# Both attentions of a hybrid transformer block: transposes of the inverted sums placed behind the products with the values

## The chip, the cores and the metric

The kernel runs on one core of a Trainium2 chip. The metric is the device time of one execution in microseconds (us); the time before is the median of three runs. A profile of one execution comes with it. Its engines are TensorE (PE for matmuls, PEld for the loading of their weights), VectorE (DVE), ScalarE (ACT), GpSimd (POOL) and SyncE (SP, which here only issues DMAs). Every engine works through its own queue in the order of the program and waits at an instruction until what it needs is there.

## What is computed

A transformer block on 1024 tokens of width 1024, with 256 context tokens, all in float32. After a norm and one wide projection there are two attentions with 8 heads of width 64 each, whose results are gated, projected and added to the input; a mixture of 16 experts follows.

```python
def _attend(q, k, v, scale):                       # latent attention, all 1280 keys
    s = jnp.einsum('bqhd,bkhd->bhqk', q, k).astype(jnp.float32) * scale
    p = jax.nn.softmax(s, axis=-1).astype(v.dtype)
    return jnp.einsum('bhqk,bkhd->bqhd', p, v)
...
# local attention: a window of 8 x 16 tokens on a 16 x 64 grid, and the context
p = jax.nn.softmax(jnp.concatenate([s_loc, s_ctx], axis=-1), axis=-1).astype(v.dtype)
return (jnp.einsum('bhqk,bqkhd->bqhd', p[..., :nk], v_win)
        + jnp.einsum('bhqk,bkhd->bqhd', p[..., nk:], v_ctx))
```

Both softmaxes are left undivided in the kernel: the products with the values run on the bare exponentials, and their result is multiplied by the inverse of the sums.

## The kernel before

The program is written out by hand in the order in which each engine shall take it. Its stages are: norm and input projections (to about 480 us), the local attention (`na_attention`, to about 662 us), the latent attention (`ml_attention`, to about 940 us), output projection with gates, norm and router, and the experts (from about 1180 us).

Both attentions go over 64 units; a unit is one head and 128 queries. Unit n's scores stand in a score tile (`pS`, two of them). `soft` takes their maximum on VectorE (L767 to L773 in the local attention, L887 to L889 in the latent one) and the exponential on ScalarE (L775; L891 and L892), which also gives the row sum. `transp` brings the exponentials (queries by keys) into keys by queries: 128x128 transposes on TensorE into tiles `pT` and `pY`, from which ScalarE (L788, L800, L802; L912) and, for the last two key blocks of the latent attention, VectorE (L914) evacuate them. `pv` multiplies with the values: the output has the head's 64 columns as partitions and the queries as columns, so two heads stand one above the other in one tile (64-column weights; L815 local, L927 latent).

The scale of a query is then needed as a row, the same on 64 partitions. For that `inverses` takes the reciprocal of the sums and spreads each over 64 columns on VectorE (L716, L718); `rows_of` transposes this on TensorE (L724) into spare columns of the products' own tile, and ScalarE copies the result back to the buffer `inv` (L725), by which VectorE multiplies the products (L819 local, L934 latent).

One step n of either loop issues: the inverses (every fourth step), the scores of unit n + 2, the transposes of unit n, every fourth step `pv` for the four units before, the rest of the evacuations, `soft` of unit n + 2, and the scaling. In the local attention a fourth step has two `pv` of a pair of units each, the first into the tile `pM`, the second into `pY`; in the latent attention it has one `pv` for two heads and 256 queries, into `pY`, of which there is one buffer and which the last transposes of the other three units use too. `pv` puts the transposes of the inverses first, then the products; the copy stands behind the products in the program of the local attention and ahead of them in the latent one.

The last step of the latent attention (n = 64) has no unit of its own. What follows on ScalarE is the first split of the projection (`split`, L86, with its remainder on VectorE, L87): weights and attention results are each parted into a rounded value and a remainder. The gated products of the projection are taken on VectorE (L1157); the loads of gates (L1086, L1087) and of the next weights (L1014) stand behind one another in SP's queue.

Of the kernel before, what the change touches and what calls it, by code (L numbers as in the profile page):

```python
# [9 lines left out]
F32 = mybir.dt.float32  # L10
# [17 lines left out]
def block_kernel(ctx, tc, a, out, dbg=None):  # L28
# [6 lines left out]
    def pool(st, name, side=None, **kw):  # L35
        return st.enter_context(tc.tile_pool(name=name, bufs=kw.pop("bufs", 1), side=side, reuse_waits="tile", **kw))
# [37 lines left out]
    def ps_S():  # L74
        return psum[0].tile([128, psum[4]], F32, name="pS", bufs=psum[1])

    def ps_T():
        return psum[0].tile([128, 512], F32, name="pT", bufs=psum[2])

    def ps_Y():  # L80
        return psum[0].tile([128, 512], F32, name="pY", bufs=psum[3])
# [7 lines left out]
    def mm3(ps, ahi, alo, bhi, blo, first, last):  # L89
        nc.tensor.matmul(ps, ahi, bhi, start=first, stop=False)  # L90
        nc.tensor.matmul(ps, ahi, blo, start=False, stop=False)  # L91
        nc.tensor.matmul(ps, alo, bhi, start=False, stop=last)  # L92
# [564 lines left out]
    for it, (kind, c) in enumerate(order):  # L657
# [4 lines left out]
        n = T if kind in "qg" else N  # L662
# [43 lines left out]
    yp = pool(yst, "y", side="right")  # L706
# [7 lines left out]
    def inverses(r, n):  # L714

        nc.vector.reciprocal(r, r)  # L716
        w = p.tile([128, n, 64], F32, name=f"inv{n}", bufs=2)
        nc.vector.tensor_copy(w, r[:, :, None].to_broadcast([128, n, 64]))  # L718
        return w.rearrange("p n c -> p (n c)")

    def rows_of(w, ps, dst=None):

        for i in range(0, w.shape[1], 128):
            nc.tensor.transpose(ps[:, i:i + 128], w[:, i:i + 128], ident)  # L724
        return lambda: nc.scalar.activation(w if dst is None else dst, ps, AF.Copy)  # L725
# [4 lines left out]
    def ps_M():  # L730
        return psum[0].tile([128, 512], F32, name="pM")

    def na_attention(then):

        units = [(2 * c + h, j) for c in range(4) for j in range(8) for h in range(2)]
        S, Pm, PT, RS, PT2 = {}, {}, {}, {}, {}

        def geo(j):
            R0 = min(max(2 * j - 4, 0), 8)
            rows = 9 if 2 <= j <= 5 else 8  # L740
            return R0, rows
# [62 lines left out]
        def pv(n0, inv):  # L804

            c, j = units[n0][0] // 2, units[n0][1]
            R0, rows = geo(j)
            py = ps_Y() if n0 % 4 else ps_M()
            copy = rows_of(inv, py[:, 128:256])
            kts = [8, 9] + [R0 // 2 + i for i in range(4)] + ([R0 // 2 + 4] if rows == 9 else [])  # L810
            for i, kt in enumerate(kts):
                kk = 64 if i == 6 else 128
                for h in range(2):
                    col = (2 * c + h) * 64
                    nc.tensor.matmul(py[h * 64:(h + 1) * 64, 0:128], vna[0:kk, kt, col:col + 64],  # L815
                                     PT[n0 + h][0:kk, i], start=(i == 0), stop=(i == len(kts) - 1))
            PT.pop(n0), PT.pop(n0 + 1)
            copy()
            return lambda: nc.vector.tensor_tensor(yT[:, 4 + c, j * 128:(j + 1) * 128], py[:, 0:128], inv, op=OP.mult)  # L819

        nu = len(units)
# [43 lines left out]
    def ml_attention():  # L865
        units = [(2 * c + h, 2 * g + i) for c in range(4) for g in range(4) for h in range(2) for i in range(2)]
        S, Pm, PT, RS = {}, {}, {}, {}

        def score(n):
            h, j = units[n]  # L870
            o = heads[8 + h]
            ps = ps_S()
            smid[0] = smid[0] or ps_M()
            mid = smid[0][:, (n % 2) * 256:(n % 2 + 1) * 256]
            q = slice(j * 128, (j + 1) * 128)
            for c0, c1 in ((0, 512), (512, 1024), (1024, N)):
                mm3(ps[:, c0:c1] if c0 < 1024 else mid, o["qh"][:, q], o["ql"][:, q], o["kh"][:, c0:c1], o["kl"][:, c0:c1], True, True)
            S[n] = ps, mid

        def soft(n):  # L880
            ps, mid = S.pop(n)
            sm = p.tile([128, 3], F32, name="sn", bufs=6)
            g, h, i = n // 4, n // 2 % 2, n % 2
            if n % 4 == 0:
                RS[g] = p.tile([128, 2, 4], F32, name="st", bufs=3)
            total = RS[g][:, :, 2 * i + h:2 * i + h + 1]
            nc.vector.tensor_reduce(sm[:, 0:1], ps, axis=AX.X, op=OP.max)  # L887
            nc.vector.tensor_reduce(sm[:, 1:2], mid, axis=AX.X, op=OP.max)
            nc.vector.tensor_scalar(sm[:, 2:3], sm[:, 0:1], sm[:, 1:2], -MLA_SCALE, op0=OP.max, op1=OP.mult)  # L889
            pm = p.tile([128, N], F32, name="pm", bufs=3)  # L890
            nc.scalar.activation(pm[:, T:], mid, AF.Exp, bias=sm[:, 2:3], scale=MLA_SCALE, accum_out=total[:, 0])  # L891
            nc.scalar.activation(pm[:, :T], ps, AF.Exp, bias=sm[:, 2:3], scale=MLA_SCALE, accum_out=total[:, 1])  # L892
            Pm[n] = pm

        tb = {}

        def transp(n, b):
            tb[b] = ps_Y() if b == 2 and (n % 4 or n == 0) else ps_T()
            k0, k1 = ((0, 4), (4, 8), (8, 10))[b]
            for k in range(k0, k1):  # L900
                nc.tensor.transpose(tb[b][:, (k - k0) * 128:(k - k0 + 1) * 128], Pm[n][:, k * 128:(k + 1) * 128], ident)  # L901

        def evac(n, b):
            g, i = divmod(n, 4)
            h = i // 2
            if b == 0 and i % 2 == 0:
                PT[g, h] = p.tile([128, 2560], F32, name="pt", bufs=4).rearrange("p (k q) -> p k q", q=256)
            k0, k1 = ((0, 4), (4, 8), (8, 10))[b]
            dst = PT[g, h][:, k0:k1, (i % 2) * 128:(i % 2 + 1) * 128]
            src = tb.pop(b)[:, :(k1 - k0) * 128].rearrange("p (k q) -> p k q", q=128)  # L910
            if b < 2:
                nc.scalar.activation(dst, src, AF.Copy)  # L912
            else:
                nc.vector.tensor_copy(dst, src)  # L914

        py = [None]

        def pv(g):
            c = g // 4
            py[0] = ps_Y()  # L920
            dst = RS[g] if g < 15 else yp.tile([128, 256], F32, name="inv")
            rows_of(RS[g], py[0][:, 256:512], dst)()
            RS[g] = dst
            for k in range(10):
                for h in range(2):
                    col = (2 * c + h) * 64
                    nc.tensor.matmul(py[0][h * 64:(h + 1) * 64, 0:256], vm[:, k, col:col + 64], PT[g, h][:, k],  # L927
                                     start=(k == 0), stop=(k == 9))

        def scaled(g):  # L930

            r, y, c = RS.pop(g), py[0], g // 4
            PT.pop((g, 0)), PT.pop((g, 1))
            return lambda: nc.vector.tensor_tensor(yT[:, c, (g % 4) * 256:(g % 4 + 1) * 256], y[:, 0:256], r, op=OP.mult)  # L934

        def start(n):
            score(n)
            soft(n)

        na_attention(start)  # L940
        if "yna" in dbg:
            nc.sync.dma_start(dbg["yna"], yT[:, 4:8])
        nu = len(units)
        for n in range(nu + 1):
            on = 0 <= n < nu
            if on:
                c, i = divmod(n, 16)
                if i in (0, 7) and c < 3:
                    todo.extend(ml_prep(2 * c + 2 + (i == 7)))
                if n + 2 < nu and units[n + 2][0] // 2 != units[n][0] // 2:  # L950
                    while todo:
                        todo.pop(0)()
            if n >= 4 and n % 4 == 0:
                r = RS[n // 4 - 1]
                nc.vector.tensor_tensor(r[:, 0], r[:, 0], r[:, 1], op=OP.add)
                RS[n // 4 - 1] = inverses(r[:, 0], 4)
            if n + 2 < nu:
                score(n + 2)
            if on:
                for b in range(2):  # L960
                    transp(n, b)
                    evac(n, b)
            out = None
            if n >= 4 and n % 4 == 0:
                pv(n // 4 - 1)
                out = scaled(n // 4 - 1)
            if on:
                transp(n, 2)
            if n + 2 < nu:
                soft(n + 2)  # L970
            if on:
                evac(n, 2)
                Pm.pop(n)
            if out:
                last.append(out)
                if n // 4 - 1 < 15:
                    last.pop()()
            if todo:
                todo.pop(0)()
# [977 lines left out]
```

## Time and profile before

| | us |
|---|---|
| median of three runs | 1809.28 (1805.93, 1809.28, 1815.73) |
| the profiled execution | 1804.39 |
| its span, first to last instruction | 1802.6 |
| TensorE busy in the span | 1682.8 (93%) |
| VectorE busy | 1176.6 (65%) |
| ScalarE busy | 927.9 (51%) |
| GpSimd busy | 596.4 (33%) |
| local attention | about 484 to 662 |
| latent attention | about 664 to 940 |

Matmuls are pipelined and their ends are modelled, so a busy TensorE is not TensorE at its peak. The share of busy time is an average over stages with different limits; what a change in one stage is worth is read in that stage. In the rows below, a bracket at the end of a row of the timeline gives the time for which the engine sat idle before it, and what ended that; rows of several like instructions are merged and carry their count.

### The profile page before, as it was taken

How to read it: one execution, taken by the hardware profiler on the slowest of the kernel's cores; microseconds unless marked ns; L12 is line 12 of the kernel's file. 1: busy time of each engine (PE TensorE's matmuls, PEld its weight loads, DVE VectorE, ACT ScalarE, POOL GpSimd, SP SyncE). 2: the span in 40 equal slices, each digit the busy share in tenths (PEclk: the TensorE clock that was granted, in tenths of full speed). 3: DMA queues.
4: the chain of work that ended last, by engine and by line, in shares of the span. 5: the costliest groups of instructions: out<-in, count | busy, mean ns of one | idle time of the engine just before them, and what ended most of it. 6: DMA issues, size and time to landing. Idle time of an engine off the chain costs nothing. (4 is left out here: it accounts for less than half of the span.)

```text
span 1802.6 us, 25426 instructions
## 1 busy us (share of the span) xinstructions
PE 1682.8 (93%) x9607; PEld 1340.9 (74%) x9609; DVE 1176.6 (65%) x1860; ACT 927.9 (51%) x1477; POOL 596.4 (33%) x488
## 2 busy tenths in 40 slices
PE   5999999999899999999989999788999999999996
PEld 3778778897777777777767776546887887888872
DVE  5612143203477766656555587887999999999986
ACT  3422222112366666667670032245777777777774
POOL 0334555543244422112000101256333433443135
PEclk9999999999999999999999999889999999999998
DMA  8334545255334311000025643877999999999944
GB/s 327 108 115 142 214 164 204 85 133 145 102 80 87 72 36 40 21 21 21 1 82 159 211 164 152 319 286 272 367 380 370 392 388 379 374 387 394 369 163 187
DMA packets 96891, 356.63 MB, mean 198 GB/s; under 512 B 28368, under 2 KB 36944, under 8 KB 70912
## 3 DMA queue, kind: packets, MB, share of 16 engines
q1 hardware_dynamic: 78032, 285.78, 43.9%
q0 software_dynamic: 11376, 41.42, 7.7%
q10 hardware_dynamic: 7360, 27.81, 3.9%
q8 instruction: 75, 1.23, 0.3%
q14 instruction: 48, 0.39, 0.1%
HBM read 312.85 MB, written 42.12 MB: 197 GB/s over the span
## 5 line engine op out<-in xcount | busy, mean ns | idle before, releaser
L1711 DVE TENSOR_TENSOR hl<-raw,hl 128x1024 fp32r<-128x1024 f32 x177 | 214.8, 1241 | 21.8 <-ACT hl L1710 19.9
L1710 ACT ACTIVATE hl<-raw 128x1024 fp32r<-128x1024 f32 x182 | 187.9, 1057 | 39.8 <-PE pgate L92 19.2
L405 PE MATMUL pS<-uhi,whi 128*128 128x512 f32 (+1 forms) x440 | 131.0, 386 | 2.9 <-DVE stg L492 2.2
L1607 POOL TENSOR_SCALAR oh<-iot,slot 128x128 bf16<-128x128 f32 x112 | 133.3, 1206 | 0.5
L87 DVE TENSOR_TENSOR wlo<-raw,whi 128x1024 fp32r<-128x1024 f32 x25 | 35.8, 1434 | 145.5 <-ACT whi L86 145.5
L405 PE MATMUL pS<-uhi,wlo 128*128 128x512 f32 (+1 forms) x440 | 129.3, 383 | 0.0
L405 PE MATMUL pS<-ulo,whi 128*128 128x512 f32 (+1 forms) x440 | 129.1, 382 | 0.0
L310 POOL TENSOR_TENSOR sb<-qs,sa 128x512 fp32r<-128x512 f32 x28 | 35.9, 1283 | 265.3 <-DVE sa L309 132.9
L1710 ACT ACTIVATE whl<-raw 128x1024 fp32r<-128x1024 f32 x91 | 96.5, 1060 | 39.3 <-PE pgate L92 19.0
L1864 POOL DMA_INDIRECT acc_d<-ye,idx x15 | 35.1, 2341 | 243.1 <-DVE ye L1858 243.1
L1711 DVE TENSOR_TENSOR whl<-raw,whl 128x1024 fp32r<-128x1024 f32 x88 | 108.5, 1233 | 9.1 <-ACT whl L1710 7.8
L1711 DVE TENSOR_TENSOR raw<-raw 128x1024 fp32r<-128x1024 f32 x89 | 108.8, 1223 | 6.1 <-ACT raw L1710 6.0
L912 ACT ACTIVATE pt<-pT 128x512 f32<-128x512 f32 x128 | 69.5, 595 | 81.6 <-PE pT L901 78.4
L380 POOL TENSOR_TENSOR rawm<-rawm,scol 128x1024 f32<-128x1024 f32 x32 | 65.5, 2048 | 132.1 <-DMA rawm<-in_w_mod_dram 132.1
L1710 ACT ACTIVATE raw<-raw 128x1024 fp32r<-128x1024 f32 x91 | 96.3, 1058 | 19.8 <-PE pup L92 7.3
L1237 PE MATMUL pS<-raw,hl 128*128 128x512 f32 x384 | 96.0, 399 | 1.6 <-DVE t L1157 1.1
L887 DVE TENSOR_REDUCE sn<-pS 128x1 f32<-128x1024 f32 x64 | 78.3, 1223 | 27.7 <-PE pS L92 27.1
L405 PEld LDWEIGHTS pS<-uhi,whi 128*128 128x128 f32 x440 | 79.1, 189 | 22.8 <-issue 3.9
L405 PEld LDWEIGHTS pS<-uhi,wlo 128*128 128x128 f32 x440 | 80.4, 189 | 16.3
L405 PEld LDWEIGHTS pS<-ulo,whi 128*128 128x128 f32 x440 | 80.2, 188 | 16.5
L927 PE MATMUL pY<-pt,v 128*64 128x256 f32 x640 | 72.6, 382 | 10.5 <-ACT inv L725 10.5
L1237 PEld LDWEIGHTS pS<-raw,hl 128*128 128x128 f32 x384 | 69.7, 188 | 16.9 <-ACT cb L1329 1.5
(493 smaller groups left out, 4688.6 us busy)
## 6 DMA issues: line engine op xcount, KB each, us to landing
raw<-in_w_exp_gate_dram SPq DMA_DIRECT2D x64, 1024.0 KB
raw<-in_w_exp_up_dram SPq DMA_DIRECT2D x64, 1024.0 KB
raw<-in_w_exp_down_dram SPq DMA_DIRECT2D x64, 1024.0 KB
rawm<-in_w_mod_dram POOLq DMA_DIRECT2D x32, 512.0 KB, 3.9
raw<-in_w_in_dram SPq DMA_DIRECT2D x25, 512.0 KB
wm<-in_w_mod_dram SPq DMA_DIRECT2D x8, 1024.0 KB
sig_d<-stg ACTq DMA_DIRECT2D x16, 512.0 KB
sg<-sig_d SPq DMA_DIRECT2D x32, 256.0 KB
```

Source lines behind the costliest of these rows:

```text
L87: eng.tensor_tensor(lo, src, hi.bitcast(F32), op=OP.subtract)
L310: lo_engine[0].tensor_tensor(lo[:, cs], src[p0:p1, cs], hi[p0:p1, cs].bitcast(F32), op=OP.subtract)
L380: nc.gpsimd.tensor_tensor(raw, raw, scol[:, :, 0:1].to_broadcast([128, KT, 128]), op=OP.mult)
L405: nc.tensor.matmul(pt[:, c0:c1], ww[:, kt], uu[:, kt, c0:c1], start=(kt == 0 and k == 0), stop=(kt == KT - 1 and k == 2))
L887: nc.vector.tensor_reduce(sm[:, 0:1], ps, axis=AX.X, op=OP.max)
L912: nc.scalar.activation(dst, src, AF.Copy)
L927: nc.tensor.matmul(py[0][h * 64:(h + 1) * 64, 0:256], vm[:, k, col:col + 64], PT[g, h][:, k], start=(k == 0), stop=(k == 9))
L1237: nc.tensor.matmul(ps[b], x[:, kt], w[:, kt % 4], start=(kt == 0 and k == 0), stop=(kt == 7 and k == 2))
L1607: nc.gpsimd.tensor_scalar(ohb[:, t], iot, slot[:, t, e:e + 1], None, op0=OP.is_equal)
L1710: nc.scalar.activation(w[:, 0], src, AF.Copy)
L1711: lo_on(e, i).tensor_tensor(w[:, 1], src, w[:, 0].bitcast(F32), op=OP.subtract)
L1864: nc.gpsimd.indirect_dma_start(out=acc_d[:, :], out_offset=bass.IndirectOffsetOnAxis(ap=idx[:, :1], axis=0), in_=ye, in_offset=None, compu ...
```

## The change

In the local attention the transposes of the inverses move from ahead of a pair's products to behind them; the copy stays behind both. In the latent attention the transposes move behind the products too, and the copy, which stood between transposes and products, moves to the end of the step: behind `soft` of unit n + 2 and the evacuation L914, just ahead of the scaling. No instruction is added or removed.

```diff
@@ na_attention, pv
             py = ps_Y() if n0 % 4 else ps_M()
-            copy = rows_of(inv, py[:, 128:256])
...
             PT.pop(n0), PT.pop(n0 + 1)
-            copy()
+            rows_of(inv, py[:, 128:256])()
@@ ml_attention, pv
             py[0] = ps_Y()
-            dst = RS[g] if g < 15 else yp.tile([128, 256], F32, name="inv")
-            rows_of(RS[g], py[0][:, 256:512], dst)()
-            RS[g] = dst
             for k in range(10):
...
+            dst = RS[g] if g < 15 else yp.tile([128, 256], F32, name="inv")
+            copy = rows_of(RS[g], py[0][:, 256:512], dst)
+            RS[g] = dst
+            return copy
@@ ml_attention, step n
-                pv(n // 4 - 1)
+                copy = pv(n // 4 - 1)
                 out = scaled(n // 4 - 1)
...
             if out:
+                copy()
                 last.append(out)
```

## Rows read from the trace of the kernel before

**Rows 1.** Both attentions: stretch, its length, busy time (count) per engine, clock, DMA.

```profile
484.00:662.00 178.00, 162.43 (x1619) 136.53 (x1618) 133.43 (x364) 120.28 (x309) 71.03 (x49) 1.00 0.32 69
664.00:934.00 270.00, 255.44 (x1837) 204.83 (x1835) 164.67 (x339) 179.23 (x399) 44.37 (x34) 1.00 0.10 28
```

**Rows 2.** Waits, latent attention: engine, tile, line, releaser; us in all, times, longest.

```profile
PEld pY L927 <- ACT inv L725: 13.6, 15, 1.0
...
PE pY L927 <- ACT inv L725: 10.0, 15, 0.8
...
PEld pY L724 <- PE pT L901: 3.3, 6, 0.6
```

**Rows 3.** Timeline, one group: start, us, engine, line, operation, idle before and its releaser.

```profile
800.38 1.22 DVE L887 TENSOR_REDUCE sn<-pS 128x1 f32<-128x1024 f32 x1
...
801.18 1.08 ACT L912 ACTIVATE pt<-pT 128x512 f32<-128x512 f32 x2
801.30 0.25 PEld L724 LDWEIGHTS pY<-ident,inv 128*128 128x128 f32 x2
...
802.15 0.39 ACT L725 ACTIVATE inv<-pY 128x256 f32<-128x256 f32 x1
...
802.59 4.08 PEld L927 LDWEIGHTS pY<-pt,v 128*64 128x64 f32 x40 [1.03 <-ACT inv L725]
...
802.86 1.14 ACT L892 ACTIVATE pm<-pS,sn 128x1024 f32<-128x1024 f32 x1
...
807.06 0.20 PEld L901 LDWEIGHTS pT<-ident,pm 128*128 128x128 f32 x2 [0.39 <-issue]
...
807.53 0.43 DVE L914 COPY pt<-pT 128x256 f32<-128x256 f32 x1 [5.34 <-PE pT L901]
...
807.87 0.41 DVE L934 TENSOR_TENSOR yT<-pY,inv 128x256 f32<-128x256 f32 x1
...
809.85 0.25 PEld L901 LDWEIGHTS pY<-ident,pm 128*128 128x128 f32 x2
```

**Rows 4.** Waits of TensorE in the local attention.

```profile
PE pM L724 <- DVE inv L718: 5.8, 5, 1.3
PE pS L754 <- ACT pm L775: 5.8, 22, 0.4
...
PE pY L724 <- DVE inv L718: 1.1, 3, 0.4
```

**Rows 5.** Timeline of one step with products in the local attention.

```profile
581.60 0.33 PE L724 MATMUL pM<-ident,inv 128*128 128x128 f32 x1 [1.21 <-DVE inv L718]
...
585.09 0.15 DVE L773 TENSOR_SCALAR sm<-sm 128x1 f32<-128x1 f32 x1
...
585.47 0.19 PEld L754 LDWEIGHTS pS<-sc,sa 128*128 128x128 f32 x1 [0.17 <-issue]
...
585.59 0.28 ACT L725 ACTIVATE inv<-pY 128x128 f32<-128x128 f32 x1 [1.88 <-PE pY L815]
...
586.18 0.94 ACT L775 ACTIVATE pm<-pS,sm 128x832 f32<-128x832 f32 x1
...
587.27 0.19 PEld L754 LDWEIGHTS pS<-sc,sa 128*128 128x128 f32 x1 [0.27 <-ACT pm L775]
```

**Rows 6.** Timeline, last group of the latent attention and start of the projection.

```profile
934.17 0.42 DVE L914 COPY pt<-pY 128x256 f32<-128x256 f32 x1 [2.24 <-PE pY L901]
...
936.07 0.62 ACT L86 ACTIVATE hl<-raw 128x512 fp32r<-128x512 f32 x1
...
936.23 4.08 PEld L927 LDWEIGHTS pY<-pt,v 128*64 128x64 f32 x40 [0.71 <-ACT inv L725]
...
936.73 0.69 DVE L87 TENSOR_TENSOR hl<-raw,hl 128x512 fp32r<-128x512 f32 x1 [1.52 <-ACT hl L86]
```

**Rows 7.** The chain that ended last, at the projection's start: start, us, what.

```profile
950.25 1.15 DVE t L1157
...
954.63 6.81 DMA raw<-in_w_proj_dram
```


## The prediction

> **What bounds the kernel now.** I read the stretches first: what each engine does in the local attention (the loop over `na_attention`, about 484 to 662 us) and in the latent attention (`ml_attention`, 664 to 934 us). In both TensorE is the busiest engine by far, 162.4 of 178 us and 255.4 of 270 us, always at the full granted clock [rows 1]. So a gain must come out of TensorE's 14.6 us of idle time in the second stretch and 15.6 us in the first; nothing in the change takes work from it. Then the list of waits tells what TensorE idles for, and the timeline of one group shows the order of the steps.
>
> In the latent attention nearly all of it stands at one place. Fifteen times the weight loads of the values' product (L927) wait for ScalarE's copy of the inverted sums (L725), 13.6 us in all (the matmuls' own idle time is put at 10.0, but their ends are modelled, and weight loads show when the queue went on, so I count those); six times the transposes of the sums (L724) also come late, 3.3 us of weight-load gap, because VectorE has not yet spread the inverses [rows 2]. One group shows it: the two transposes of the sums are issued at 801.30, right behind the unit's own; ScalarE is busy with the two evacuations L912 until 802.26 and takes the copy at 802.15, and only at 802.59 do the products start, after 1.03 us without a weight load [rows 3].
>
> In the local attention TensorE idles for two things: for VectorE's spread inverses (5.8 us in five places, 1.1 us in three), and 5.8 us in 22 places because the next scores (L754) need a score tile that ScalarE's exponential (L775) has not yet released [rows 4]. Its units run almost as fast as ScalarE allows.
>
> **The change, latent attention.** Nothing is removed: 16 groups keep their two transposes, one copy and 40 product passes. The products now stand first. What they read, the probabilities of the four units before, was evacuated in the step before, so they can start when the unit's own transposes have been issued. The gap of 13.6 + 3.3 = 16.9 us [rows 2] goes, except for what TensorE takes to change from a whole 128-column array to 64-column halves. That change is not visible ahead of the product today, since it lies inside the wait. Its nearest rows are the other way round: 0.17 us after 128-column products [rows 5] and 0.39 us after 256-column ones [rows 3]. The transposes before the product have 128 columns, so I take 0.17: 15 x 0.17 = 2.6, and 16.9 - 2.6 = **14 us** for the fifteen groups inside the loop. Bounds: 16.9 with no drain, 16.9 - 15 x 0.39 = 11 with the long one. The switch behind the product is paid once now (to the transposes of the unit) and once after (to the transposes of the sums).
>
> *A rule weighed here.* The products write other columns of the tile than the copy reads, and still they begin 0.05 us after its end (802.54 to 802.59) [rows 3]. The Trainium skill, "PSUM — Partial Sum Buffer", section "PSUM bank collisions raise a hardware error", says that two engines must be kept apart by bank and not by address; the trace agrees, and by that rule the new order has no such wait left, as ScalarE reads the bank after TensorE's last write. Against the change speaks "TensorEngine Tiling (Array Packing)", section "Key Properties" of the Trainium skill: changing the tiling mode drains TensorE. By it every switch costs a drain of what is in flight, which is the first rival below.
>
> What the copy's new place costs: ScalarE takes it behind the exponentials of the unit after next. Those run until about 804.0, and the product's end is near 806.7 today [rows 3], some 0.9 us earlier afterwards, so ScalarE is idle when the transposes of the sums come, and the copy follows them by about 0.4 us. On VectorE, L914 comes first and takes 0.43 us after the unit's last transposes, as now; the scaling L934 then finds the copy done (transposes, then 0.39 us of copy, against transposes, L914's wait and its 0.43). L934 frees the tile pY, the only buffer of its kind, for the next unit's last transposes, and ends at 808.28, 1.57 us before they start [rows 3]. Queued behind L934 on VectorE are the next unit's maxima, which wait for scores anyway. Cost: none, hidden by that 1.57 us. SP's and POOL's queues are not passed: no DMA belongs to the moved step.
>
> **The change, local attention.** The wait for the inverses, 5.8 + 1.1 = 6.9 us [rows 4], moves behind a product of some 2 us, where the inverses are ready. But what is late next? In three of the five places the two waits stand together, as 1.21 us at 581.60 and some 0.37 us more at the second transpose (a third of the 1.1 [rows 4]). There VectorE is late itself: its last step for the next exponential, L773, ends at 585.24, and the exponential starts at 586.18 [rows 5]. It can move up by 0.94 us, not by 1.58. So three places give 3 x 0.94 = 2.8, the others the rest, 6.9 - 3 x 1.58 = 2.2: 5.0 us. Against it: the second copy now waits for a transpose that stands behind the second product. Today the copy starts 0.12 us after the scores that follow (585.59 against 585.47). Afterwards the transpose ends 0.33 us after its start, of which its weight load (half of the 0.25 us for two [rows 3]) lies ahead of the scores, and the copy follows: about 0.24 us. These 0.12 us go into the chain copy, evacuations, exponential, release of the score tile, on which TensorE waits for 0.27 us already [rows 5]: 16 x 0.12 = 1.9 us. Net **3 us** gained; bounds -1.9 and +6.9.
>
> **The change, last group.** Its copy stands at the end of ScalarE's work for the attention, ahead of the splits for the projection (L86). Today the copy is taken before the product, and L86 starts at 936.07 while TensorE multiplies. Afterwards the product starts when L914 has ended (934.59), takes 4.08 us of weight loads and the 0.39 us of switching, to 939.1; transposes and copy take about 0.7 us more, and L86 starts near 939.8: 3.7 us later [rows 6]. VectorE follows ScalarE's first split without a gap until the first gated product L1157 at 950.25, and that stands on the chain that ended last: from it SP's queue goes on to the load of the next projection weights at 954.63 [rows 7]. So the last group **loses 3.8 us** on the path, with nothing to hide it (0 if the projection had slack, which the chain denies).
>
> **Sum.** -14 - 3 + 3.8 = -13.4 us (rounded from 3.1). The profiled execution has 1804.4 us (span 1802.6), so 1791.0. The median of the three runs is 1809.3, 4.9 us above the profiled one: on that scale 1796. Behind the projection everything waits for what came before it, and its loads start by released tiles, so I see nothing that gives the gain back.
>
> **Rivals.** (1) *The drain takes part of the wait's place.* Each switch ahead of the product costs 0.39 us, not 0.17: 11 - 3.8 + 3.1 = 10.4 us gained, 1799. For it: the row after the products. Against it: what drains there has twice the columns. (2) *The last group's delay is hidden*: 17.2 us gained, 1792. For it: the chain through the projection is mostly the latency of loads, which vary. Against it: VectorE has no gap between the splits and L1157. (3) *The change does not do what it says*: the products wait for ScalarE's evacuations L912 of the same unit, and the copy was only the last thing that ScalarE signalled. They end at 802.26, the products would start near 802.3, and the sums' transposes (0.25 us) come on top afterwards: nothing gained in the latent attention, +3.8 - 3.1, so 1810. Against it: the products read earlier units only, and the copy's end and their start agree to 0.05 us. (4) *Slower: the copy comes too late for pY.* If the exponentials ended after the transposes of the sums, copy and L934 would slip, and with them the release of pY. It decides from a delay of 1.57 us. Maxima and exponentials of one unit lie between 800.38 and 804.00, 3.6 us; if VectorE began them only when the product ends, the copy would be 3.6 us late and hold TensorE for 2 us in each of 15 groups: 30 - 13.4 = 17 us slower, 1826. Against it: VectorE has been idle for 5.34 us when L914 comes, and the exponentials end well ahead [rows 3].
>
> **Chances.** The forecast 0.60, (1) 0.11, (2) 0.14, (3) 0.10, (4) 0.05. A measurement of this kernel tells about 0.5% (9 us) from no change, so the border is near 1800. The forecast lies 4 us inside, and one sixth of it falls outside by the bounds of the local attention; (1) lies at the border and is halved. Faster: 0.50 + 0.055 + 0.14, about 0.70; same 0.25; slower 0.05. The range from 1787 to 1807 takes in the bounds (16.9 + 3.1 gained without the last group's loss gives 1789; 11 - 1.9 - 3.8 gives 1804, and the runs scatter by some us), and leaves out (3) and (4).
>
> **What would show it.** In the profile after: L927 no longer waits for L725; the weight-load gap ahead of it is near 0.17 us; L724 has no wait for L718; the latent attention's stretch is about 14 us shorter; in the local attention, L754's wait for L775 grows; the first L86 of the projection starts behind the last product. The prediction is wrong if L927 waits for L912, if L934 holds up VectorE, or if the projection's start has not moved against the last product.

## The result, and the profile after

| | before | after |
|---|---|---|
| median, us (8 runs each, one after the other) | 1813.03 (1805.93 to 1818.2) | 1797.61 (1792.52 to 1805.51) |
| profiled execution, us | 1804.39 | 1792.52 |
| its span, us | 1802.6 | 1790.7 |
| local attention, us | 179.50 | 176.19 |
| of it, from the scores of unit 6 on, us | 168.03 | 163.68 |
| latent attention, us | 274.36 | 260.05 |
| last scores of the latent attention to the first L86 on ScalarE, us | 7.30 | 11.09 |
| last scores to the first gated product, us | 21.40 | 25.19 |
| first gated product to the end of the span, us | 852.4 | 854.0 |

The ratio of the times is 0.9928, with an interval from 0.9902 to 0.9953: 0.72% faster, some 13 us (8.5 to 17.8 by the interval). The medians lie 15.4 us apart, inside that interval. The stages are measured in the timeline between fixed instructions: the local attention from the first weight load of its scores (L754) to the last one (L755), the latent attention from there to the last weight load of its scores (L92). The forecast was 14 and 3 us less in the two attentions and 3.8 us more at the entry to the projection; measured are 14.3, 3.3 (4.3 at the same granted clock, see the local attention below) and 3.8. In the kernel after, some lines have moved: the local product is L814 (before L815) and its scaling L818 (L819); in `ml_attention` the values' product is L923 (before L927), the unit's transposes L900 (L901), the evacuations L911 and L913 (L912 and L914), maxima and exponentials L886 to L891 (L887 to L892), the gated product L1158 (L1157). L724, L725, L754, L773, L775, L86, L87 and L934 stand where they stood.

The same two stretches as in [rows 1], in the kernel after (stretch, its length, busy time and count of PE, PEld, DVE, ACT, POOL, granted clock, DMA):

```profile
484.00:659.00 175.00, 161.42 (x1627) 136.45 (x1626) 133.86 (x369) 120.49 (x311) 71.47 (x49) 1.00 0.32 70
661.00:920.00 259.00, 255.93 (x1861) 206.73 (x1861) 165.66 (x343) 181.40 (x399) 44.36 (x34) 1.00 0.11 32
```

In the latent attention TensorE is now busy for 255.93 of 259 us: its 14.6 us of idle time are down to 3. In the local attention the idle time is still 13.6 us.

**The latent attention.** Its waits after, 661 to 920 us, against [rows 2] (engine, tile, line, releaser; us in all, times, longest):

```profile
ACT inv L725 <- PE pY L724: 28.2, 15, 2.5
...
PEld pY L724 <- issue: 5.8, 15, 0.4
...
PEld pY L923 <- issue: 2.5, 15, 0.2
...
PEld pY L923 <- DVE pt L913: 0.8, 1, 0.8
```

The wait of the product for the copy (13.6 us) and that of the sums' transposes (3.3 us) are gone from the list. What stands ahead of the product is 2.5 us in fifteen places, 0.17 each. The first row is the wait's mirror image: now ScalarE waits for TensorE, 28.2 us in all, with nothing else to do. One group in the timeline, against [rows 3] (start, us, engine, line, operation; idle before and its releaser in brackets):

```profile
791.53 4.08 PEld L923 LDWEIGHTS pY<-pt,v 128*64 128x64 f32 x40 [0.17 <-issue]
...
793.78 0.20 ACT L891 ACTIVATION_READ_ACCUMULATOR pm<-pS,sn 128x1 f32 x1
...
796.00 0.20 PEld L724 LDWEIGHTS pY<-ident,inv 128*128 128x128 f32 x2 [0.39 <-issue]
...
796.17 0.25 PEld L900 LDWEIGHTS pT<-ident,pm 128*128 128x128 f32 x2
...
796.48 0.38 ACT L725 ACTIVATE inv<-pY 128x256 f32<-128x256 f32 x1 [2.50 <-PE pY L724]
...
796.70 0.42 DVE L913 COPY pt<-pT 128x256 f32<-128x256 f32 x1 [4.47 <-PE pT L900]
...
797.04 0.41 DVE L934 TENSOR_TENSOR yT<-pY,inv 128x256 f32<-128x256 f32 x1
```

Read from the top: the product starts 0.17 us behind the unit's own transposes. ScalarE ends the exponentials at 793.98, and stands ready 2.50 us before the transposes of the sums let its copy start (796.48). The copy ends (796.86) while L913 is running, and L934 follows L913 without a gap, as it did before.

**The local attention.** TensorE's waits after, 484 to 659 us, against [rows 4], and one step, against [rows 5]:

```profile
PE pS L754 <- ACT pm L775: 10.1, 32, 0.8
PE pT L787 <- ACT pt L788: 1.6, 2, 1.0
PE pY L724 <- DVE inv L718: 0.8, 3, 0.4
```

```profile
582.98 0.33 PE L724 MATMUL pY<-ident,inv 128*128 128x128 f32 x1 [0.21 <-DVE inv L718]
...
583.35 0.28 ACT L725 ACTIVATE inv<-pY 128x128 f32<-128x128 f32 x1 [1.72 <-PE pY L724]
...
584.32 0.15 DVE L773 TENSOR_SCALAR sm<-sm 128x1 f32<-128x1 f32 x1
...
584.57 0.95 ACT L775 ACTIVATE pm<-pS,sm 128x832 f32<-128x832 f32 x1 [0.52 <-DVE sm L773]
...
585.66 0.19 PEld L754 LDWEIGHTS pS<-sc,sa 128*128 128x128 f32 x1 [1.09 <-ACT pm L775]
```

The wait for the inverses (L724) fell from 6.9 us to 0.8, that of L787 is none of the change's work, and the wait for the exponential's release of the score tile grew from 5.8 to 10.1. The step shows why: at 584.57 the exponential itself has waited 0.52 us for VectorE (L773), and TensorE pays 1.09 us for it at 585.66.

The stage's length holds something that is not the change's work. All that is issued before the scores of unit 6 comes ahead of the first moved instruction. Up to the start of these scores, and from there to its end, the stage took (kernel before, then after; columns as in the first fence, the granted clock behind POOL's count):

```profile
474.91:486.38 11.47, 8.67 (x62) 7.31 (x60) 8.55 (x25) 8.42 (x18) 3.07 (x3) 1.00 0.13 52
486.38:654.41 168.03, 154.59 (x1536) 130.20 (x1537) 128.99 (x350) 113.64 (x293) 69.59 (x48) 1.00 0.34 72
```

```profile
475.26:487.76 12.50, 9.78 (x62) 8.84 (x60) 8.56 (x25) 8.48 (x18) 3.06 (x3) 0.86 0.13 46
487.76:651.45 163.69, 152.62 (x1536) 129.25 (x1537) 127.97 (x350) 112.59 (x293) 69.68 (x48) 1.00 0.34 74
```

The same work at the start takes 1.03 us more in the kernel after, where the granted clock is 0.86, a mix of the two levels of 2.4 and 1.2 GHz. Behind it, at 1.00 in both, the stage is 4.3 us shorter. TensorE had waited 1.41 us for an exponential just before in both kernels; why the clock fell in one alone is not known. It goes with the execution and not with the order: the start takes 11.5 us at 1.00 in before and the kernels 2, 3 and 6 to 10 below, and 12.2 to 12.5 us at 0.86 in after and in 1, 4, 5, 11 and 12.

**The last group.** Timeline at the entry to the projection, against [rows 6], and the chain there (start, us, what), against [rows 7]:

```profile
916.88 0.42 DVE L913 COPY pt<-pY 128x256 f32<-128x256 f32 x1 [2.23 <-PE pY L900]
...
917.36 4.08 PEld L923 LDWEIGHTS pY<-pt,v 128*64 128x64 f32 x40 [0.76 <-DVE pt L913]
...
921.83 0.20 PEld L724 LDWEIGHTS pY<-ident,inv 128*128 128x128 f32 x2 [0.39 <-issue]
...
922.31 0.38 ACT L725 ACTIVATE inv<-pY 128x256 f32<-128x256 f32 x1 [5.05 <-PE pY L724]
922.59 0.62 ACT L86 ACTIVATE hl<-raw 128x512 fp32r<-128x512 f32 x1
...
923.24 0.69 DVE L87 TENSOR_TENSOR hl<-raw,hl 128x512 fp32r<-128x512 f32 x1 [5.32 <-ACT hl L86]
```

```profile
936.77 1.15 DVE t L1158
...
942.52 5.35 DMA raw<-in_w_proj_dram
```

ScalarE sits idle for 5.05 us while TensorE multiplies, because the copy heads its queue, and the splits L86 stand behind it; VectorE's L87 waits 5.32 us for them. The gated product comes at 936.77, 13.5 us sooner than before (950.25), and the load that follows on the chain lands 11.1 us behind it, before 11.2: what the two attentions gave and the last group took is handed on unchanged there.

### The profile page after: what moved, and what is told of

The parts are those of the page before. It is cut to its first block, busy times and chain, and to the rows that moved or that the text cites. A ratio compares the mean times of both kernels' runs of the same rounds, so it can differ in the third digit from the quotient of the medians.

```text
span 1790.7 us, 25352 instructions
## 1 busy us (share of the span) xinstructions
PE 1676.3 (94%) x9609; PEld 1337.7 (75%) x9609; DVE 1174.9 (66%) x1860; ACT 928.5 (52%) x1477; POOL 591.8 (33%) x488
## 5 line engine op out<-in xcount | busy, mean ns | idle before, releaser
L87 DVE TENSOR_TENSOR wlo<-raw,whi 128x1024 fp32r<-128x1024 f32 x25 | 36.5, 1463 | 143.0 <-ACT whi L86 142.9
L886 DVE TENSOR_REDUCE sn<-pS 128x1 f32<-128x1024 f32 x64 | 78.3, 1223 | 27.4 <-PE pS L92 26.7
L911 ACT ACTIVATE pt<-pT 128x512 f32<-128x512 f32 x128 | 69.5, 595 | 34.3 <-PE pT L900 31.0
L1238 PEld LDWEIGHTS pS<-raw,hl 128*128 128x128 f32 x384 | 69.7, 188 | 17.6 <-ACT cb L1330 1.5
L900 PE MATMUL pT<-ident,pm 128*128 128x128 f32 x542 | 72.2, 273 | 1.3 <-ACT pt L911 1.3
```

Of the source, the lines that this page charges most:

```text
L1238: nc.tensor.matmul(ps[b], x[:, kt], w[:, kt % 4], start=(kt == 0 and k == 0), stop=(kt == 7 and k == 2))
```

## The experiments

Each kernel ran beside the kernel before on the same chip; stages are measured as in the table above. In us, for all of them:

| kernel | local | latent | last scores to L86 | to the gated product | span |
|---|---|---|---|---|---|
| before | 179.50 | 274.36 | 7.30 | 21.40 | 1802.6 |
| after | 176.19 | 260.05 | 11.09 | 25.19 | 1790.7 |
| 1 local part alone | 176.15 | 274.35 | 7.29 | 21.39 | 1802.7 |
| 2 latent part alone | 179.51 | 259.92 | 11.09 | 25.19 | 1797.3 |
| 3 copy straight behind the transposes | 175.10 | 259.94 | 11.09 | 25.19 | 1800.9 |
| 4 last group in the old order | 175.81 | 259.93 | 7.55 | 21.65 | 1786.8 |
| 5 before, transposes in another tile | 180.57 | 267.73 | 7.55 | 21.65 | 1798.7 |
| 6 copy held back by two copies | 175.09 | 260.13 | 11.04 | 25.14 | 1789.7 |
| 7 by five copies | 175.09 | 300.73 | 14.55 | 28.65 | 1838.7 |
| 8 local copies behind the exponential | 177.84 | 259.88 | 11.09 | 25.19 | 1801.7 |
| 9 last copy behind the splits | 175.63 | 259.93 | 5.66 | 19.77 | 1792.2 |
| 10 local copies behind the evacuations | 174.00 | 259.98 | 11.09 | 25.19 | 1791.7 |
| 11 9 and 10 together | 175.02 | 259.95 | 5.67 | 20.12 | 1790.8 |
| 12 the changed kernel again | 176.66 | 260.01 | 11.09 | 25.19 | 1797.3 |

Among the kernels with the changed latent order the latent attention repeats to 0.3 us (all but 1, 5 and 7); among those with the changed local order the local one repeats to 1.6 us (after, 1, 3, 4, 6, 7, 9, 12), of which 1.0 is the start at the lower clock. From the scores of unit 6 on, the local attention takes 168.0 to 168.1 us in the old order (before, 2, 5), 163.6 to 163.7 in the new one (after, 1, 3, 4, 6, 7) and 164.2 in 9 and 12, 166.4 in 8, and 162.5 in 10 and 11. Spans don't sort these kernels, as the part behind the first gated product takes from 852.4 to 864.3 us in these profiles, and 854.0 and 860.5 in after and 12, which are one program (last section). Of 5, 6 and 7 there is one execution each, so only their stages are read.

**1 and 2: the two parts by themselves.** Kernel before with one hunk of the diff each: first the one in `na_attention`, then the two in `ml_attention`.

```diff
@@ 1, na_attention, pv (against before)
-            copy = rows_of(inv, py[:, 128:256])
...
-            copy()
+            rows_of(inv, py[:, 128:256])()
@@ 2, na_attention, pv (against after)
+            copy = rows_of(inv, py[:, 128:256])
...
-            rows_of(inv, py[:, 128:256])()
+            copy()
```

> Only the local attention has the new order; the latent one is as before. Theory: the two stretches are independent, so the local attention (first scores L754 to the last ones) takes 176.2 us as in the changed kernel, against 179.5 before (-3.3), the latent attention stays at 274.4, the projection's first split follows the last scores by 7.3 us as before. Time -3 us, ratio 0.998. Rival (the last group's delay is hidden, and the local attention brings all that the latent one does not): no other length moves, but the time falls by more than 6 us.

> Only the latent attention has the new order. Theory: the local attention stays at 179.5 us, the latent one falls from 274.4 to 260 us (-14.3), and the first split of the projection stands 11.1 us behind the last scores instead of 7.3 (+3.8). Time -10 us, ratio 0.994. Rival (the gain is a matter of the whole, such as the phase of the loads behind): the latent attention shortens by less than 10 us when the local one is as before.

Measured: the local part shortens the local attention by 3.3 us and nothing else; the latent part shortens the latent one by 14.4 and lengthens the entry by 3.8, and leaves the local one at 179.51. The parts add up. In time, 1 gives a ratio of 0.9964 (0.9949 to 0.998). The 3.3 us of its profile are 0.18% of 1814 us, just outside the interval; but its start ran at the lower clock too, and the 4.4 us from unit 6 on are 0.24%, inside it. 2 gives 0.9947 (0.9928 to 0.9966), which is the 10.6 us of its stages (0.58%).

**3: is it the order on TensorE, or the copy's last place?** The copy follows the transposes at once, ahead of the exponentials of the unit after next.

```diff
@@ ml_attention, pv
-            copy = rows_of(RS[g], py[0][:, 256:512], dst)
+            rows_of(RS[g], py[0][:, 256:512], dst)()
...
-            return copy
@@ ml_attention, step n
-                copy()
```

> The changed kernel, but in the latent attention the copy stands straight behind the transposes of the sums in the program, ahead of the exponentials of the unit after next, instead of at the end of the step. ScalarE then waits 5 us for the product before it takes the exponentials. Theory: the product's early start is the whole gain; the exponentials end some 2.7 us after the transposes of the sums, about when ScalarE's next evacuations become due (2.7 us after them), so the latent attention takes 260 to 264 us. Rival (the gain comes from the exponentials being taken 0.4 us earlier, with the copy out of their way): the latent attention goes back to 270 us or more.

Measured: 259.94, as after; ratio 0.9912 (0.9895 to 0.9928). The timeline of one group there:

```profile
796.89 0.20 PEld L724 LDWEIGHTS pY<-ident,inv 128*128 128x128 f32 x2 [0.39 <-issue]
...
797.36 0.38 ACT L725 ACTIVATE inv<-pY 128x256 f32<-128x256 f32 x1 [4.18 <-PE pY L724]
...
798.09 1.12 ACT L891 ACTIVATE pm<-pS,sn 128x1024 f32<-128x1024 f32 x1
...
799.75 1.09 ACT L911 ACTIVATE pt<-pT 128x512 f32<-128x512 f32 x2 [0.45 <-PE pT L900]
```

The exponentials now wait for TensorE and run late, to 799.30, but ScalarE still has 0.45 us to spare before the next evacuation. So the whole gain of the latent part comes from the transposes' place on TensorE, and the copy's last place brings nothing; it only keeps more slack.

**4: the last group in the old order.** Fifteen groups stay changed; the last has transposes and copy ahead of its product.

```diff
@@ ml_attention, pv
+            if g == 15:
+                dst = yp.tile([128, 256], F32, name="inv")
+                rows_of(RS[g], py[0][:, 256:512], dst)()
+                RS[g] = dst
             for k in range(10):
...
+            if g == 15:
+                return lambda: None
```

> The changed kernel, but the last of the sixteen groups of the latent attention has the old order (transposes, copy, products). Theory: ScalarE is free for the projection's splits before the last product, so the first split stands 7.3 us behind the last scores as before, instead of 11.1, and everything behind it comes 3.8 us earlier: time 3.8 us under the changed kernel, 17 us under the one before, ratio 0.990. Rival (the last group's delay is hidden by the loads of the projection): the first split moves, but the first gated product and the time stay where they are in the changed kernel.

Measured: L86 starts 7.55 us behind the last scores instead of 11.09, and the gated product comes 3.5 us sooner, with the latent attention as short as after. The time is 1789.58, ratio 0.9876 (0.9855 to 0.9898), some 22 us under the kernel before by the ratio, where 17 were expected; the stages show the 3.5 us and not the rest. Behind the gated product it takes 854.9 us (after 854.0). So the 3.8 us at the entry are on the path, and they are the last group's. Not expected: its product ran at half the granted clock. Three stretches of it (columns as in the first fence above; the granted clock stands behind POOL's count):

```profile
917.00:920.00 3.00, 2.53 (x12) 1.35 (x13) 1.52 (x3) 2.46 (x6) 0.00 (x0) 0.50 0.61 210
920.00:923.00 3.00, 3.00 (x16) 1.66 (x14) 3.00 (x6) 3.00 (x6) 0.00 (x0) 0.51 0.09 33
923.00:926.00 3.00, 3.00 (x23) 1.91 (x20) 3.00 (x6) 3.00 (x6) 0.00 (x0) 1.00 0.00 0
```

0.50 and 0.51 are 1.2 GHz, the lower of the two levels; the kernel before, with the same order in its last group, shows 1.00 from 915 to 941 us. It cost almost nothing: from 920 us on VectorE and ScalarE, with the splits, are busy throughout, and the gated product comes only 0.25 us later behind the last scores than before (21.65 against 21.40).

**5: what did the product wait for?** The kernel before, with the transposes of the sums in a tile of the unit's transposes instead of spare columns of pY.

```diff
@@ ml_attention, pv (against before)
-            rows_of(RS[g], py[0][:, 256:512], dst)()
+            rows_of(RS[g], ps_T()[:, 0:256], dst)()
```

> The kernel before, with one edit: in the latent attention the transposes of the sums go to a tile of the pT ring instead of into spare columns of the products' own tile. Order and copy are as before. Theory (the products waited because the copy reads the tile that they write): they no longer wait for the copy and follow the transposes after the switch of 0.17 us. The transposes wait instead until ScalarE's first evacuation has released a pT tile, near 0.45 us, so the latent attention shortens by 0.4 to 0.5 us per group, some 6 us, to about 268 us. Rival (ScalarE's queue sets the product's start, wherever the copy reads): it stays at 274 us.

Measured: 267.73 in the latent attention, where 268 was expected. A group of it:

```profile
797.97 0.20 PEld L724 LDWEIGHTS pT<-ident,inv 128*128 128x128 f32 x2 [0.49 <-ACT pt L912]
...
798.34 1.71 PEld L927 LDWEIGHTS pY<-pt,v 128*64 128x64 f32 x18 [0.17 <-issue]
...
798.45 0.38 ACT L725 ACTIVATE inv<-pT 128x256 f32<-128x256 f32 x1
```

The product starts at 798.34, ahead of the copy (798.45), with the transposes in the same place as before. So the old wait was for the shared tile, and not for the values that the copy makes. The Trainium skill, "PSUM — Partial Sum Buffer", section "PSUM bank collisions raise a hardware error", tells to guard by bank and not by address: the trace agrees as far as it goes, since the wait leaves with the tile (here) or with the order (after); tile and bank are not told apart by these runs. This cure gives only half of the gain, since the transposes now wait 0.49 us for a tile that the evacuations L912 still hold.

**6 and 7: how much delay does the copy bear?** The kernel after, with ScalarE copies of 128 x 1024 elements into an unused tile ahead of the copy, in the fifteen groups inside the loop: two in 6, five in 7. This is added work; the rest is unchanged.

```diff
@@ ml_attention, step n
             if out:
+                if on:
+                    junk = p.tile([128, 1024], F32, name="junk")
+                    for _ in range(2):
+                        nc.scalar.activation(junk, vm[:, 0:2].rearrange("p t c -> p (t c)"), AF.Copy)
                 copy()
```

> The changed kernel with two extra copies of 128x1024 on ScalarE (1.06 us each) ahead of the copy of the sums, in the fifteen groups inside the loop. Theory: ScalarE idles 2.5 us there, so 2.1 us more are hidden: latent attention 260 us. Rival (the copy is on the path): 15 x 2.1 = 32 us more, 292 us.

> The same with five extra copies, 5.3 us: the copy of the sums comes 2.8 us late. Theory: from 1.57 us on, the scaling releases pY too late for the next unit's last transposes, so TensorE waits about 1.2 us per group, 18 us in fifteen, latent attention 278 us; some more if VectorE's maxima, queued behind the scaling, hold the exponentials too. Rival (pY and the queue behind the scaling have more room than the rows of before showed): under 265 us.

Measured: two copies (2.14 us together) vanish in ScalarE's idle time, 260.13. Five cost 41 us, to 300.73, where 278 was expected. The waits of 7 from 661 to 952 us:

```profile
DVE yT L934 <- ACT inv L725: 45.4, 15, 3.9
ACT pm L890 <- DVE sn L888: 27.7, 22, 1.6
...
PE pY L900 <- DVE yT L934: 20.2, 15, 2.2
...
PEld pM L90 <- ACT pm L890: 14.2, 17, 1.2
```

The mechanism of the fourth rival is there: L934 waits for the copy, pY is released late, and TensorE's transposes into it wait 20.2 us, 1.35 us a group where 1.2 had been worked out. The other half was named in the expectation, without a price. The next unit's maxima stand behind L934 on VectorE, so the exponentials wait 27.7 us for them (after 12.8) and the scores for the exponentials (14.2 us; after 4.1). The granted clock also falls, to 0.84 from 770 to 790 us and 0.91 from 830 to 870, where the kernel after has 1.00 in both; how the rest of the 41 us divides between the late maxima and the clock was not separated.

**8: local copies behind the exponential.** If ScalarE's chain were what sets the local attention, both copies of a pair should go to the end of its work.

```diff
@@ na_attention, pv
-            rows_of(inv, py[:, 128:256])()
-            return lambda: nc.vector.tensor_tensor(...)
+            copy = rows_of(inv, py[:, 128:256])
+            return copy, lambda: nc.vector.tensor_tensor(...)
@@ behind the exponential
-                for job in scaled:
+                for copy, _ in scaled:
+                    copy()
+                for _, job in scaled:
```

> The changed kernel, but in the local attention too both copies come last: behind the evacuations and the exponential of the unit after next, just ahead of the scaling. Theory (the copies hold ScalarE until the second product ends, and the exponential behind them holds the next scores): the exponential runs during the products, TensorE's wait for it (L754 for L775, 11.5 us in the changed kernel) falls to a half or less, the local attention takes about 170 us instead of 176.2, ratio to before 0.989. Rival (VectorE, late with the maxima, is what holds the exponential): 175 us or more.

Measured: 177.84 in the local attention, 1.7 us longer than after (2.7 from unit 6 on) instead of some 6 us shorter; ratio 0.9923 (0.9895 to 0.9952). Its waits from 484 to 656 us:

```profile
ACT pm L775 <- DVE sm L773: 37.3, 34, 4.3
DVE yT L818 <- ACT inv L725: 23.9, 22, 1.6
...
PE pS L754 <- ACT pm L775: 15.8, 20, 1.5
```

The theory falls and the rival holds: the exponentials wait 37.3 us for L773 (4.5 after). In sum the scaling L818 waits for the copy about as long as after (23.9 us against 23.3), but the copy now stands behind the exponential, so L818 is taken later, and the maxima of the next unit stand behind it on VectorE.

**9: the last copy behind the splits.** Nothing moves but the last group's copy, which goes where its scaling already is, behind ScalarE's first splits for the projection.

```diff
@@ ml_attention, step n
-                copy()
-                last.append(out)
+                last.append(lambda: (copy(), out()))
```

> The changed kernel, but the last group's copy stands just ahead of its scaling, behind most of the projection's splits, instead of ahead of them; its products stay in front of its transposes. Theory (the last copy holds ScalarE for the 5 us that the product takes): the first split starts when the last evacuation ends, some 5 us earlier, 6 us behind the last scores instead of 11.1; the first gated product comes 5 us earlier too, and so does the end: 18 us under the kernel before, ratio 0.990. Rival (from there on TensorE's last product or the weights' load holds the projection): the gated product gains no more than the 3.5 us that the old order of the last group gave.

Measured: the first L86 starts 5.66 us behind the last scores, 5.4 sooner than after and 1.6 sooner than before, and the gated product too comes 5.4 us sooner. Ratio 0.9902 (0.9876 to 0.9928), beside 0.9932 for the changed kernel on the same chip. Its timeline:

```profile
913.90 0.62 ACT L86 ACTIVATE hl<-raw 128x512 fp32r<-128x512 f32 x1
...
918.57 0.20 PEld L724 LDWEIGHTS pY<-ident,inv 128*128 128x128 f32 x2 [0.39 <-DVE hl L87]
...
922.13 0.36 ACT L725 ACTIVATE inv<-pY 128x256 f32<-128x256 f32 x1
...
928.01 1.21 DVE L1157 TENSOR_TENSOR t<-pS,sg 128x1024 f32<-128x1024 f32 x1
```

L86 starts before the sums' transposes exist, and the copy is taken 3.6 us behind them, and it costs at most the 0.53 us for which the last split then waits for the scaling L934.

**10: local copies between.** The copies go behind the evacuations of the second transposes and ahead of the exponential; `pv` returns them as in 8.

```diff
@@ na_attention, behind the evacuations of the second transposes
+            if four:
+                for copy, _ in scaled:
+                    copy()
...
-                for job in scaled:
+                for _, job in scaled:
```

> The changed kernel, but in the local attention both copies stand behind the evacuations L800 and L802 of the unit and ahead of its exponential, instead of ahead of both. The scaling and VectorE's queue keep their place against the copies. Theory (behind the second product the chain copy, evacuations, exponential, score tile sets the next scores): 0.6 us less stands between the copy and the exponential in each of 16 steps, and TensorE's wait for the score tile falls by a third to a half: local attention 171 to 173 us instead of 175.1 to 176.2. Rival (VectorE's maxima set the exponential, as in the run with the copies last): no shorter than 175 us.

Measured: 174.00, between what the two theories say (173 at most, 175 at least); ratio 0.992 (0.9894 to 0.9945). TensorE's wait for the exponential did not fall (10.2 us, after 10.1), and the exponentials' wait for VectorE rose from 4.5 to 7.1 us:

```profile
PE pS L754 <- ACT pm L775: 10.2, 21, 0.8
ACT pm L775 <- DVE sm L773: 7.1, 20, 0.9
```

The whole stage does not decide it, as kernel 11, with the same local order, has 175.02 and a start at the lower clock. From unit 6 on both have 162.5 us, and the order of after 163.6 to 164.2: the new place gains 1.1 to 1.6 us, not the 2 to 5 of the theory, and the longer wait for VectorE is where at least a part of the rest goes.

**11 and 12: both last edits, and the changed kernel again.** 11 joins the diffs of 9 and 10; 12 is the kernel after, word for word.

> Both edits at once: in the local attention the copies behind the evacuations, and the last copy of the latent attention behind the projection's splits. Theory: the lengths add, local 171 to 173 us, latent 260, first split 6 us behind the last scores; 21 us under the kernel before, ratio 0.988. Rival (what the projection gains at its start is lost in its chain of loads): the time is that of the changed kernel within 2 us.

> The changed kernel itself beside the three others on the same chip. Ratio to before 0.993; local attention 175 to 176.2 us, latent 260, first split 11.1 us behind the last scores.

Measured: 11 has 1790.31 us, ratio 0.9893 (0.9863 to 0.9923); 12 has 1799.65, ratio 0.9932 (0.9906 to 0.9959). In its stages 11 misses the local length (175.02, expected 171 to 173) and has the early entry (5.67). In 12 the local attention is 0.5 us above the expected range, with its start at the lower clock. Kernels 4, 9 and 11 have lower medians than the changed kernel (11 by 9.3 us against 12, which speaks against its rival), but only the interval of 4 lies clear of those of after and 12; which of them is best stays open. The stages point to 11: from unit 6 on its local attention is 1.6 us shorter than that of 9, and its gated product comes 0.35 us later behind the last scores.

## Why the prediction was right

**The latent term** (14; measured 14.3). Both gaps went, and in their place came the switch, at the value that was taken from a row of the other direction: 0.17 us ahead of each product, 15 times, 2.5 us. 13.6 + 3.3 - 2.5 = 14.4. The first rival (0.39 each) falls by that row, and with it the lower bound of 11. The Trainium skill, "TensorEngine Tiling (Array Packing)", section "Key Properties", says that a change of the tiling mode drains TensorE; the trace agrees, at 0.17 us behind matmuls of 128 columns and 0.39 behind those of 256.

**The copy costs nothing** (by the cover of 1.57 us). It held. ScalarE was idle for 2.50 us when the transposes came, kernel 6 puts 2.14 us there for nothing, and kernel 7 shows what it costs when that cover is gone. The fourth rival named the right mechanism and was unlikely for the right reason, the margin. Its price counted the late release of pY alone; in kernel 7 the whole cost is twice that, with the maxima behind L934 as a part of the difference and the lower clock as a possible other.

**The third rival** (products really wait for the evacuations) falls: after, the product starts at 791.53, while the evacuations of the same unit are running, and kernel 5 shows it for the old order.

**The local term** (3.1; measured 3.3 in the stage, 4.3 at the same granted clock). That 3.3 lies so near 3.1 is luck: the lower clock at the start took 1.0 us of the gain. The steps of the sum are right, with one term too large. From the first scores of one step with products to those of the next (fifteen such stretches), before against after, the three steps where both waits stood gain 0.80, 0.82 and 0.81 us, where 0.94 - 0.12 = 0.82 was forecast: the cap by L773 holds. The two others with a wait gain 1.07 and 1.27, 2.3 us where 2.2 - 0.24 = 2.0 was forecast. The ten without lose 0.4 us in all instead of 1.2: six lose 0.09 to 0.16 each, which fits the 0.12 of the copy's later start, three change by 0.05 at most, and one gains 0.29. So the term of 1.9 was the one mis-sized.

The copy's start was not varied by itself; with the copies behind the evacuations (kernel 10), three of those six steps gain 0.12 to 0.14 us instead. L754's wait for the exponential was forecast to grow by 1.9 + 1.9 = 3.8 us and grew by 4.3. Three transposes still wait 0.21 to 0.4 us for L718, 0.8 us in all, where the text had none left. In TensorE's weight loads from unit 6 on, the wait for the inverses fell by 7.9 us, that for the exponential grew by 4.0 and the other gaps by 0.5; 1.0 of the 4.3 us stands in no gap.

**The last group** (+3.8; measured +3.8). The first split moved from 936.07 to 922.59, 13.5 us, while the two attentions gave 17.6; of the rest 3.8 is the copy at the head of ScalarE's queue, and 0.3 that the local attention began later. The second rival (hidden) falls by kernels 4 and 9, which take it away and get the gated product 3.5 and 5.4 us sooner. From there to the first matmul of the experts it is 231.0 to 234.8 us in all these kernels (after 233.0, 4 has 233.7, 9 has 234.7), so most of that arrives there.

**The sum.** As they are rounded, its terms (14 or 14.3, 3 or 3.1, 3.7 or 3.8) give 13.2 to 13.7, for the 13.4 that it states. 1796 was forecast and 1797.6 measured, and a part of that nearness is chance: the forecast counts from 1809.28, and the kernel before has 1813.03 over eight runs. The gain is the better measure, 13.4 against some 13 by the ratio and 15.4 between the medians; in the profiled executions it is 11.9. Of these, 13.5 us are there at the gated product, and 1.6 are missing behind it. The text saw nothing there that gives the gain back. The scatter behind the projection, below, is larger than 1.6 us, so this is no loss that can be pinned on the change.

## What to carry to other kernels

A product that must wait for an unrelated copy, only because both use one accumulator tile, is cured by order: put the side work behind the accumulation, and see whether the engine that does the copy is idle there. At the end of a loop the same order can be wrong, because an instruction that heads an in-order queue holds up the next stage behind it; treat the last iteration by itself. When one wait is taken away, read which engine's step ends next (here VectorE's maxima), as it caps the gain.

## What the runs showed of the hardware

Executions of one program differ: the eight of the kernel after run from 1792.52 to 1805.51 us. The profiles place much of it in the experts' stage: from the first to the last matmul of L90 that takes `hl` and `xh` into `pgate` it is 566 us before and after and in kernels 1, 4, 5 and 6, 569 to 571 in 2, 7 and 10, 574 to 575 in 3, 8, 9, 11 and 12. The kernel after and its repetition (12) are the same program. Stretches of 10 us from the first of these matmuls on, the second one of after, then the second and third of 12 (columns as in the first fence):

```profile
1189.40:1199.40 10.00, 7.24 (x29) 4.12 (x27) 6.56 (x10) 4.99 (x7) 5.48 (x3) 1.00 0.83 294
```

```profile
1188.20:1198.20 10.00, 5.36 (x17) 4.07 (x16) 6.79 (x14) 2.41 (x3) 5.40 (x3) 0.70 0.81 310
1198.20:1208.20 10.00, 7.70 (x38) 4.45 (x38) 5.05 (x14) 3.53 (x6) 0.00 (x0) 0.84 0.47 154
```

Where TensorE is busy for 7.24 of 10 us in one execution and for 5.36 in the other, the granted clock stays at 1.00 in the first and falls to 0.70, then 0.84, in the second. Its two levels are 1.2 and 2.4 GHz, so 0.70 is a mix of both. Why it falls in one and not in the other isn't known; nor was it tried whether the fall makes the 8 us between them or only goes with the idle time around it. In kernel 4 it fell to 0.50 behind 1.42 us without a weight load, and in the kernel before, with the same order, it did not. For a change worth a few us this means: compare the stage that was edited, and not the span, and look at its granted clock first, as the start of the local attention shows: 1.0 us at 0.86 hid a quarter of the local gain.
